# Feed-forward up-projection by Strassen's seven block products, two weight slabs at a time

## The chip, the cores and the metric

The kernel runs on one core of a Trainium2 chip. The metric is device time of one execution in microseconds; the runs shown here have a median of 1751.15 us.

## The reference

One step of a streaming encoder of two layers. Its 512 prompt frames and 64 sample frames are computed together as 576 token columns, D_MODEL = 1024. Layer 0 mixes tokens by chunked band attention, layer 1 by a Mamba-2 scan; each is followed by a dense feed-forward part with 4096 hidden units, and each of these four sublayers by a residual and a layer norm:

```python
def _mlp(x, w_up, w_down):
    return (jnp.square(jax.nn.relu(x @ w_up)) @ w_down)
x = layer_norm(ALPHA * x + mixer(x))
x = layer_norm(ALPHA * x + _mlp(x, w_up, w_down))
```

All inputs and outputs are float32.

## The kernel before

**Layout and split.** Activations lie transposed, features on 128 partitions in 8 blocks, tokens along the free axis (`x32`, 128 x 8 x 576). Every large matrix product is done as three products of rounded halves: an operand is cast to the type fp32r (its high part), and the rest, operand minus high part, is cast too (its low part). A product of 128 outputs over a 1024-deep sum is 8 blocks x 3 terms (high by high, high by low, low by high), each in two token halves of 288: 48 matmuls. `dense` (L229) does both halves, `dense_half` (L251) one half for two weight slabs.

**Weights.** The weights come as 223 slabs of 128x1024 f32 in the order of `weight_plan` (L66). `Weights.load` (L128) takes a raw buffer (two of them, tag `wr`), issues the DMA on SP's queue, casts the high part on ScalarE (L144) and makes the low part on VectorE, or on GpSimd for slabs near the head of a stage (`pool_lo`, L146). High and low parts have NB = 6 buffers each. `get` asks for slabs up to LA = 4 ahead, `drop` tells that one is used up.

**The feed-forward stage** (`mlp`, L385). The 4096 hidden units are four groups q of eight tiles. `up(q)` makes eight tiles of 128 hidden units, each with Relu and Square on ScalarE (L392, L394), the copy that is the high part and the low part on VectorE (L395, L399). `down(q)` takes a group's eight tiles as its sum axis and adds to the residual stream, eight slabs (`resid`, L297, an add from PSUM on VectorE). The order is up 0, up 1, down 0, up 2, down 1, up 3, down 2, down 3. At the start LAG = 5 tiles are computed for the first token half, while the second half's layer norm of the stage before still runs beside them as a generator (`Side`, `layer_norm` L315) stepped by every 7 matmuls; then the same five for the second half. At the end the last LAG tiles of `down(3)` are done by halves in the same way, so that the first half's norm runs beside the second half's matmuls.

**Order.** The kernel is written in a framework that takes buffers from pools by tag, puts in the waits between engines, and sets the order of each engine's instructions when the program is built. An engine runs its own instructions in that fixed order. PSUM for the large products is two buffers of two banks each (tag `mm`).

## Time and profile before

| | us |
|---|---|
| median of 3 runs | 1751.15 (1749.54 to 1751.87) |
| the profiled execution | 1747.71 |
| its span, first to last instruction | 1745.9 |
| TensorE busy | 1698.6 (97%) |
| VectorE busy | 952.5 (55%) |
| ScalarE busy | 658.5 (38%) |
| GpSimd busy | 298.5 (17%) |

The mean granted clock of TensorE is 0.987 of full speed. Matmuls are pipelined, so TensorE's busy share is the share of time with a matmul under way; a matmul's own time (298 ns) overlaps the next. In the profile PE is TensorE, PEld its weight load, DVE VectorE, ACT ScalarE, POOL GpSimd, SP the queue that issues DMAs; L236 is line 236 of the kernel.

### The profile page before, as it was taken

The numbers are of one execution on the slowest core, as the hardware profiler recorded it, in microseconds if no ns is written. First come the engines' busy times: TensorE is split into PE (matmuls) and PEld (weight loads), VectorE is DVE, ScalarE is ACT, GpSimd is POOL, SyncE is SP. The second block draws the span as 40 slices with busy tenths as digits, with TensorE's granted clock in tenths as the row PEclk, the third lists the DMA queues.
The fourth block names the chain that finished last, engine by engine and source line by source line (L and its number), as shares of the span: only waits on it lengthen the run. The fifth ranks groups of instructions, "written<-read, shape, count | busy, mean of one in ns | idle before, by whom it ended". The sixth has DMA issues, their size and how long they took to land.

```text
span 1745.9 us, 30837 instructions
## 1 busy us (share of the span) xinstructions
PE 1698.6 (97%) x12857; PEld 1625.7 (93%) x12857; DVE 952.5 (55%) x1728; ACT 658.5 (38%) x1084; POOL 298.5 (17%) x343
## 2 busy tenths in 40 slices
PE   9999999899999999999999999999989999999995
PEld 8888888799999999988999999999989999999995
DVE  6555555853333333377875776777777333333326
ACT  5434442453122231145563563565226322313102
POOL 0000011400000000434441341344340000000011
PEclk9999999999999999999999999999989999999998
DMA  7343331122222222112432332333212222222211
GB/s 241 115 127 104 103 118 56 61 94 77 84 85 85 85 76 82 61 60 91 142 101 86 100 106 82 98 106 103 64 59 73 85 85 86 81 77 85 85 37 54
DMA packets 76922, 157.21 MB, mean 90 GB/s; under 512 B 11440, under 2 KB 40240, under 8 KB 76784
## 3 DMA queue, kind: packets, MB, share of 16 engines
q1 hardware_dynamic: 76784, 155.25, 27.7%
q8 instruction: 101, 1.65, 0.4%
q14 instruction: 37, 0.30, 0.1%
HBM read 145.80 MB, written 9.42 MB: 89 GB/s over the span
## 4 chain that ended last, share of the span: by engine, by line
PE 89%; DVE 7%; ACT 1%; issue 1%; POOL 1%; DMA 0%; POOLq 0%; DVEq 0%; SPq 0%; ACTq 0%
PE mm L236 73%; PE mm L258 3%; PE ax L596 1%; DVE tmp L332 1%; PE ax L618 1%; PE ax L901 1%; PE ax L904 1%; PE ax L567 1%; PE ax L906 1%; PE ax L292 1%; DVE x L325 1%; PE mm L247 1%; PE ax L577 1%; PE ax L282 1%; PE ax L870 1%
## 5 line engine op out<-in xcount | busy, mean ns | idle before, releaser
L144 ACT CAST wh<-wr 128x1024 fp32r<-128x1024 f32 x223 | 233.5, 1047 | 630.5 <-PE mm L236 602.8
L236 PE MATMUL mm<-xh,wh 128*128 128x288 f32 x1920 | 416.5, 298 | 0.1
L236 PE MATMUL mm<-xh,wl 128*128 128x288 f32 x1920 | 415.3, 298 | 0.0
L236 PE MATMUL mm<-xl,wh 128*128 128x288 f32 x1920 | 414.4, 297 | 0.0
L146 DVE TENSOR_TENSOR wl<-wr,wh 128x1024 fp32r<-128x1024 f32 x196 | 249.6, 1274 | 266.9 <-ACT wh L144 263.4
L236 PEld LDWEIGHTS mm<-xl,wh 128*128 128x128 f32 x1920 | 308.1, 189 | 4.1 <-issue 3.8
L236 PEld LDWEIGHTS mm<-xh,wh 128*128 128x128 f32 x1920 | 308.8, 189 | 2.7 <-issue 1.1
L236 PEld LDWEIGHTS mm<-xh,wl 128*128 128x128 f32 x1920 | 308.3, 189 | 1.4
L236 PE MATMUL mm<-hh,wl 128*128 128x288 f32 x1024 | 242.2, 298 | 0.0
L236 PE MATMUL mm<-hh,wh 128*128 128x288 f32 x1024 | 242.1, 298 | 0.0
L236 PE MATMUL mm<-hl,wh 128*128 128x288 f32 x1024 | 241.8, 297 | 0.0
L304 DVE TENSOR_TENSOR x<-x,mm 128x288 f32<-128x288 f32 (+1 forms) x112 | 65.1, 581 | 223.3 <-PE mm L236 223.0
L236 PEld LDWEIGHTS mm<-hh,wh 128*128 128x128 f32 x1024 | 173.5, 190 | 0.1
L236 PEld LDWEIGHTS mm<-hl,wh 128*128 128x128 f32 x1024 | 173.4, 190 | 0.0
L236 PEld LDWEIGHTS mm<-hh,wl 128*128 128x128 f32 x1024 | 173.3, 189 | 0.1
L146 POOL TENSOR_TENSOR wl<-wr,wh 128x1024 fp32r<-128x1024 f32 x27 | 66.7, 2472 | 440.4 <-ACT wh L144 435.2
L712 DVE SCALAR_TENSOR_TENSOR tmp<-xpad,pm,tmp 128x579 f32<-128x579 f32 x90 | 90.2, 1002 | 2.8 <-ACT tmp L710 2.0
L313 POOL TENSOR_TENSOR tmp<-x 128x288 f32<-128x288 f32 x8 | 6.8, 855 | 387.5 <-DVE x L304 384.6
L258 PE MATMUL mm<-xh,wh 128*128 128x288 f32 x240 | 71.2, 297 | 0.5 <-DVE x L304 0.5
L258 PE MATMUL mm<-xl,wh 128*128 128x288 f32 x240 | 71.4, 298 | 0.1
L258 PE MATMUL mm<-xh,wl 128*128 128x288 f32 x240 | 70.8, 295 | 0.0
L302 DVE SCALAR_TENSOR_TENSOR x<-x,mm 128x576 f32<-128x576 f32 (+1 forms) x34 | 24.4, 719 | 83.7 <-PE mm L236 83.5
(216 smaller groups left out, 2448.8 us busy)
## 6 DMA issues: line engine op xcount, KB each, us to landing
wr<-in_wts SPq DMA_DIRECT2D x223, 512.0 KB, 3.3
cumb<-cumd SPq DMA_DIRECT2D x32, 256.0 KB, 3.8
e<-expd SPq DMA_DIRECT2D x48, 64.0 KB, 3.5
tb<-in_rel SPq DMA_DIRECT2D x16, 160.0 KB, 3.7
tb<-in_rel SPq DMA_DIRECT2D x16, 144.0 KB, 3.0
ts<-in_rel SPq DMA_DIRECT2D x16, 144.0 KB, 2.9
out_k<-tmp SPq DMA_DIRECT2D x8, 288.0 KB, 2.3
out_v<-tmp SPq DMA_DIRECT2D x8, 288.0 KB, 2.1
```

The lines of the kernel that those rows point to most:

```text
L144: S.copy(hi[:, sl], raw)
L146: eng.tensor_tensor(out=lo[:, sl], in0=raw, in1=hi[:, sl].bitcast(F32), op=ALU.subtract)
L236: PE.matmul(ps[:, o:o + HALF], w, a(k)[:, t0:t0 + HALF], start=first and i == 0, stop=last and i == 2)
L247: PE.matmul(ps[:, PS0 + h * HALF:PS0 + (h + 1) * HALF], a, b[:, k, h * HALF:(h + 1) * HALF], start=k == 0 and i == 0, stop=k == 7 and i == 2)
L258: PE.matmul(o, a, b[:, k, h * HALF:(h + 1) * HALF], start=k == 0 and i == 0, stop=k == 7 and i == 2)
L282: PE.matmul(ps[0:96, j:j + 1], vv[:, 96 * j:96 * j + 96], scale_col, start=True, stop=True)
L292: PE.matmul(ps[:, 96 * j:96 * j + 96], y[:, j0 + j:j0 + j + 1].to_broadcast([96, 128]), ident[0:96, 0:96], start=True, stop=True)
L302: V.scalar_tensor_tensor(out=dst, in0=dst, scalar=ALPHA, in1=src, op0=ALU.mult, op1=ALU.add)
L304: V.tensor_tensor(out=dst, in0=dst, in1=src, op=ALU.add)
L325: V.tensor_tensor(out=r, in0=r, in1=pmu[:, 0:HALF].unsqueeze(1).to_broadcast([P, 2, HALF]), op=ALU.subtract)
L332: V.tensor_tensor(out=acc, in0=acc, in1=sq, op=ALU.add)
L712: V.scalar_tensor_tensor(out=acc, in0=xr[:, k:k + 579], scalar=col(k), in1=acc, op0=ALU.mult, op1=ALU.add)
```

## The change

The up-projection of two neighbouring slabs (256 hidden units, tokens in two halves, the sum axis in two halves of 512) is seen as a 2x2 by 2x2 block product and done with seven block products of four 128-blocks each instead of eight (a Winograd form of Strassen's scheme). The first four tiles of a stage (LAG is now 4) are still done by halves as before; the other 28 tiles of a layer are 14 pairs.

- Weight sums: the second operand slabs of a pair are made in place in the raw buffers by four GpSimd subtractions and additions of 128x512; a pair's four weight operands (three of 1024 columns, one of 512) are each split into high and low part.
- Token sums: t1 to t4 of `x32` are made once a stage, on VectorE with ScalarE casts, t2 to t4 (`combos`) as a side generator beside the second half of the first four tiles, t1 (`first_combo`) behind them, in place of the second half of blocks 0 to 3 of `xh`, `xl`.
- Results: four blocks of a pair are put together in an SBUF tile `ut` by three ScalarE copies and four VectorE adds from PSUM; three of the seven products go on accumulating in a bank that was copied or added before. Relu, Square and the split run once over 1152 columns.
- Order: up pairs and down groups interleave by `MLP_ORDER`; the last `down(3)` begins with two slabs together, their last two blocks behind.
- Buffers: NB 6 to 5, four raw buffers with DMAs issued ahead (`prefetch`), LAG 5 to 4, `pool_lo` from i-3 to i+3 instead of i+5, hidden tiles as five pair buffers instead of two groups of eight.

The diff, cut to its core:

```diff
-NB = 6
-LAG = 5
+NB = 5
+NR = 4
+LAG = 4
+HALFK = 512
 LA = 4
 PL0 = -3
-PL1 = 6
+PL1 = 4
 WARM = 7
 HE = 17
 DE = 40
-ACTM = 1
 LN_EVERY = 7
+CE = 12
...
+MLP_ORDER = (("up", 0, LAG // 2, 4), ("up", 1, 0, 1), ("down", 0, 0, 8), ("up", 1, 1, 4), ("up", 2, 0, 1),
+             ("down", 1, 0, 8), ("up", 2, 1, 4), ("up", 3, 0, 1), ("down", 2, 0, 8), ("up", 3, 1, 4),
+             ("down", 3, 0, 8))
+
+
...
+        p = [("up", layer, 0, m) for m in range(LAG)]
+        for kind, q, i0, i1 in MLP_ORDER:
+            if kind == "up":
+                p += [("ups", layer, q, i, g) for i in range(i0, i1) for g in (1, 2, 4, 3)]
+            else:
+                p += [("down", layer, q, m) for m in range(8)]
...
+            def prefetch(self):
+                while self.raw_done < min(self.raw_free + NR, self.n_raw):
+                    raw = wp.tile([P, 1024], F32, name="wr", tag="wr", bufs=NR)
+                    SY.dma_start(raw, io["wts"][self.raw_done])
+                    self.raw[self.raw_done] = raw
+                    self.raw_done += 1
 
             def load(self, upto):
-                while self.done < min(upto, len(plan)):
-                    i = self.done
-                    raw = wp.tile([P, 1024], F32, name="wr", tag="wr", bufs=2)
-                    hi, lo = self.alloc()
-                    self.fetch(i, raw, hi, lo, 0, 1024)
-                    self.t[i] = (hi, lo)
+                while self.done < min(upto, self.live + NB, len(plan)):
+                    self.prefetch()
+                    self.produce(self.done)
                     self.done += 1
 
             def alloc(self):
                 return (wp.tile([P, 1024], F32R, name="wh", tag="wh"),
                         wp.tile([P, 1024], F32R, name="wl", tag="wl"))
+
+            def split(self, i, raw, n=1024):
+                hi, lo = self.alloc()
+                S.copy(hi[:, 0:n], raw)
+                eng = GP if i in pool_lo else V
+                eng.tensor_tensor(out=lo[:, 0:n], in0=raw, in1=hi[:, 0:n].bitcast(F32), op=ALU.subtract)
+                self.t[i] = (hi, lo)
+
+            def produce(self, i):
+                p = plan[i]
+                r = self.raw_free
+                if p[0] != "ups":
+                    self.split(i, self.raw.pop(r))
+                    self.raw_free += 1
+                    return
+                r1, r2 = self.raw[r], self.raw[r + 1]
+                lo, hi = slice(0, HALFK), slice(HALFK, 1024)
+                if p[4] == 1:
+                    self.split(i, r1)
+                    GP.tensor_tensor(out=r2[:, lo], in0=r1[:, lo], in1=r2[:, lo], op=ALU.subtract)
+                elif p[4] == 2:
+                    self.split(i, r2)
+                    GP.tensor_tensor(out=r2[:, hi], in0=r2[:, hi], in1=r2[:, lo], op=ALU.subtract)
+                    GP.tensor_tensor(out=r1[:, lo], in0=r1[:, lo], in1=r2[:, hi], op=ALU.add)
+                    GP.tensor_tensor(out=r2[:, lo], in0=r1[:, hi], in1=r2[:, hi], op=ALU.subtract)
+                elif p[4] == 4:
+                    self.split(i, r1[:, lo], HALFK)
+                else:
+                    self.split(i, r2)
+                    del self.raw[r], self.raw[r + 1]
+                    self.raw_free += 2
+                    self.prefetch()
 
...
+        def dense_ks(ps, wf, ah, al, ks):
+            for k in ks:
+                wh, wl = wf(k)
+                for i, (w, a) in enumerate(((wh, ah), (wh, al), (wl, ah))):
+                    for t0 in (0, HALF):
+                        PE.matmul(ps[:, PS0 + t0:PS0 + t0 + HALF], w, a(k)[:, t0:t0 + HALF],
+                                  start=k == 0 and i == 0, stop=k == 7 and i == 2)
 
...
+                th = hpool.tile([P, 12, HALF], F32R, name="th")
+                tl = hpool.tile([P, 12, HALF], F32R, name="tl")
                 H = {}
+                T1, T2 = slice(0, HALF), slice(HALF, NT)
...
+                def combine(dh, dl, t):
+                    S.copy(dh, t)
+                    V.tensor_tensor(out=dl, in0=t, in1=dh.bitcast(F32), op=ALU.subtract)
+
+                def sums_of(kk):
+                    t = tmp().rearrange("p (a b) -> p a b", a=2)
+                    return t, slice(2 * kk, 2 * kk + 2), slice(4 + 2 * kk, 6 + 2 * kk)
+
+                def combos():
+                    for kk in range(2):
+                        t3, k1, k2 = sums_of(kk)
+                        V.tensor_tensor(out=t3, in0=x32[:, k2, T2], in1=x32[:, k1, T2], op=ALU.subtract)
+                        combine(th[:, 4 + 2 * kk:6 + 2 * kk, :], tl[:, 4 + 2 * kk:6 + 2 * kk, :], t3)
+                        yield
+                        t2, k1, k2 = sums_of(kk)
+                        V.tensor_tensor(out=t2, in0=t3, in1=x32[:, k1, T1], op=ALU.add)
+                        combine(th[:, k1, :], tl[:, k1, :], t2)
+                        yield
+                        t4, k1, k2 = sums_of(kk)
+                        V.tensor_tensor(out=t4, in0=x32[:, k2, T1], in1=t2, op=ALU.subtract)
+                        combine(th[:, 8 + 2 * kk:10 + 2 * kk, :], tl[:, 8 + 2 * kk:10 + 2 * kk, :], t4)
+                        yield
+
+                def first_combo():
+                    for kk in range(2):
+                        t1, k1, k2 = sums_of(kk)
+                        V.tensor_tensor(out=t1, in0=x32[:, k1, T2], in1=x32[:, k1, T1], op=ALU.subtract)
+                        combine(xh[:, k1, T2], xl[:, k1, T2], t1)
+
+                operands = {
+                    "b11": lambda k: (xh[:, k, T1], xl[:, k, T1]),
+                    "b21": lambda k: (xh[:, 4 + k, T1], xl[:, 4 + k, T1]),
+                    "b22": lambda k: (xh[:, 4 + k, T2], xl[:, 4 + k, T2]),
+                    "t1": lambda k: (xh[:, k, T2], xl[:, k, T2]),
+                    "t2": lambda k: (th[:, k, :], tl[:, k, :]),
+                    "t3": lambda k: (th[:, 4 + k, :], tl[:, 4 + k, :]),
+                    "t4": lambda k: (th[:, 8 + k, :], tl[:, 8 + k, :]),
+                }
+
+                def product(out, w, off, name, more=False):
+                    for k in range(4):
+                        wh, wl = (x[:, off + 128 * k:off + 128 * k + 128] for x in w)
+                        bh, bl = operands[name](k)
+                        for i, (a, b) in enumerate(((wh, bh), (wh, bl), (wl, bh))):
+                            PE.matmul(out, a, b, start=not more and k == 0 and i == 0, stop=k == 3 and i == 2,
+                                      skip_group_check=True)
+
+                def up_pair(q, i):
+                    hpair(q, i)
+                    w1, w2, w4, w3 = (W.get("ups", layer, q, i, g) for g in (1, 2, 4, 3))
+                    ab, cd = mmt(), mmt()
+                    a, b = ab[:, 0:HALF], ab[:, 512:512 + HALF]
+                    c, d = cd[:, 0:HALF], cd[:, 512:512 + HALF]
+                    ut = hpool.tile([P, 4, HALF], F32, name="ut", tag="ut", bufs=2)
+                    add = lambda dst, src: V.tensor_tensor(out=dst, in0=dst, in1=src, op=ALU.add)
+                    product(a, w1, 0, "b11")
+                    S.copy(ut[:, 0, :], a)
+                    product(b, w1, HALFK, "b21")
+                    add(ut[:, 0, :], b)
+                    W.drop()
+                    W.load(W.pos + 2)
+                    product(d, w2, 0, "t3")
+                    S.copy(ut[:, 3, :], d)
+                    product(c, w4, 0, "t1")
+                    add(ut[:, 3, :], c)
+                    product(a, w3, HALFK, "t2", True)
+                    S.copy(ut[:, 1:3, :], a.unsqueeze(1).to_broadcast([P, 2, HALF]))
+                    add(ut[:, 3, :], a)
+                    product(d, w2, HALFK, "t4", True)
+                    W.drop(2)
+                    W.load(W.pos + 4)
+                    product(c, w3, 0, "b22", True)
+                    add(ut[:, 1:3, :], cd.rearrange("p (a b) -> p a b", a=2)[:, :, 0:HALF])
+                    W.drop()
+                    W.load(W.pos + 4)
+                    u = ut.rearrange("p a b -> p (a b)")
+                    S.activation(u, u, AF.Relu)
+                    S.activation(u, u, AF.Square)
+                    hh, hl = (x.rearrange("p a b -> p (a b)") for x in H[q, i])
+                    V.tensor_copy(hh, u)
+                    V.tensor_tensor(out=hl, in0=u, in1=hh.bitcast(F32), op=ALU.subtract)
+
...
+                            side.start(combos(), CE)
...
+                    side.drain()
+                    first_combo()
...
+                        w2 = [W.get("down", layer, q, m) for m in range(2)]
+                        p2 = [mmt(), mmt()]
+                        for ks in (range(0, 6), range(6, 8)):
+                            for w, ps in zip(w2, p2):
+                                dense_ks(ps, wk(w), bh, bl, ks)
+                        for m, ps in enumerate(p2):
+                            for h in range(2):
+                                resid(ps, m, (h,), False, True)
+                            W.drop()
+                        for m in range(2, 8 - LAG):
```

## Rows read from the trace of the kernel before

**Rows 1.** The page's busy time, share and instructions of an engine.
```profile
PE 1698.6 (97%) x12857; PEld 1625.7 (93%) x12857; DVE 952.5 (55%) x1728; ACT 658.5 (38%) x1084; POOL 298.5 (17%) x343
```

**Rows 2.** Chain of waits, whole span: start us, us, what.
```profile
369.29 363.50 PE mm L236 x2726
```

**Rows 3.** Busy time by engine in the feed-forward stretch of layer 0.
```profile
369.30:732.80 363.50, 363.50 (x2727) 363.50 (x2727) 122.03 (x148) 92.00 (x112) 14.38 (x12) 1.00 0.25 83
```

**Rows 4.** Groups of instructions, 400 to 725 us (busy us, mean ns).
```profile
L146 DVE TENSOR_TENSOR wl<-wr,wh 128x1024 fp32r<-128x1024 f32 x47 | 57.6, 1226 | 93.1 <-ACT wh L144 91.7
L399 DVE TENSOR_TENSOR hl<-tmp,hh 128x576 fp32r<-128x576 f32 x23 | 17.5, 759 | 0.8
L304 DVE TENSOR_TENSOR x<-x,mm 128x576 f32<-128x576 f32 x16 | 12.1, 755 | 67.2 <-PE mm L236 67.2
L395 DVE CAST hh<-tmp 128x576 fp32r<-128x576 f32 x23 | 10.6, 461 | 1.0
L304 DVE TENSOR_TENSOR x<-x,mm 128x288 f32<-128x288 f32 x9 | 4.1, 455 | 23.1 <-PE mm L236 23.1
...
L144 ACT CAST wh<-wr 128x1024 fp32r<-128x1024 f32 x50 | 52.4, 1047 | 237.3 <-PE mm L236 237.3
L394 ACT ACTIVATE tmp<-tmp 128x576 f32<-128x576 f32 x23 | 15.8, 687 | 0.7
L392 ACT ACTIVATE tmp<-mm 128x576 f32<-128x576 f32 x23 | 14.8, 645 | 0.0
```

**Rows 5.** GpSimd's source lines: duration ns min/median/max.
```profile
L146 POOL TENSOR_TENSOR wl<-wr,wh x27: 2337/2395/2934, 249.3 to 1316.3; 128x1024 fp32r<-128x1024 f32 x27
...
L873 POOL TENSOR_TENSOR mt<-cumb,cumt x40: 606/1040/1772, 820.4 to 1238.5; 128x512 f32<-128x512 f32 x32, 64x256 f32<-64x256 f32 x8
...
L875 POOL TENSOR_TENSOR mt<-mt,negm x40: 724/1294/2139, 821.5 to 1239.2; 128x512 f32<-128x512 f32 x32, 64x256 f32<-64x256 f32 x8
```

**Rows 6.** Order of time near 313 us (start, us, instruction), line 332's durations.
```profile
312.54 2.40 POOL L146 TENSOR_TENSOR wl<-wr,wh 128x1024 fp32r<-128x1024 f32 x1 [3.43 <-ACT wh L144]
312.71 0.45 DVE L302 SCALAR_TENSOR_TENSOR x<-x,mm 128x288 f32<-128x288 f32 x1
313.08 2.47 DVE L332 TENSOR_TENSOR tmp<-tmp 128x576 f32<-128x576 f32 x1
...
L332 DVE TENSOR_TENSOR tmp<-tmp x24: 735/758/2480, 313.1 to 1731.3; 128x576 f32<-128x576 f32 x24
```

**Rows 7.** Order of time, ScalarE (in brackets idle before, releaser).
```profile
420.33 1.05 ACT L144 CAST wh<-wr 128x1024 fp32r<-128x1024 f32 x1 [4.09 <-PE mm L236]
421.28 0.64 ACT L392 ACTIVATE tmp<-mm 128x576 f32<-128x576 f32 x1
```

**Rows 8.** Order of time, TensorE and VectorE, start of layer 0's feed-forward stage.
```profile
333.36 0.29 PE L258 MATMUL mm<-xh,wh 128*128 128x288 f32 x1
347.65 0.81 PE L292 MATMUL ax<-pm,y 96*128 96x96 f32 x6
...
351.52 1.59 DVE L357 TENSOR_TENSOR xl<-x,xh 128x576 fp32r<-128x576 f32 x2
356.84 0.76 DVE L357 TENSOR_TENSOR xl<-x,xh 128x576 fp32r<-128x576 f32 x1 [0.63 <-ACT xh L356]
```

**Rows 9.** Order of time, TensorE and VectorE, layer 0's end of feed-forward.
```profile
749.19 1.12 PE L292 MATMUL ax<-pm,y 96*128 96x96 f32 x6 [2.01 <-DVE y L277]
...
753.65 0.75 DVE L357 TENSOR_TENSOR xl<-x,xh 128x576 fp32r<-128x576 f32 x1
756.87 0.75 DVE L357 TENSOR_TENSOR xl<-x,xh 128x576 fp32r<-128x576 f32 x1
```

**Rows 10.** Order of time, TensorE after a wait.
```profile
326.22 1.39 PE L292 MATMUL ax<-pm,y 96*128 96x96 f32 x6 [3.81 <-DVE y L277]
...
327.95 0.44 PE L236 MATMUL mm<-oh,wl 128*128 128x288 f32 x1
328.19 0.44 PE L236 MATMUL mm<-oh,wh 128*128 128x288 f32 x1
```

More of the change, by code (lines that the diff above doesn't have):

```diff
@@ L63, with slab_plan @@
 GORD = (("c", 0), ("z", 0), ("b", 0), ("x", 0), ("x", 1), ("z", 1))
+MLP_ORDER = (("up", 0, LAG // 2, 4), ("up", 1, 0, 1), ("down", 0, 0, 8), ("up", 1, 1, 4), ("up", 2, 0, 1),
+             ("down", 1, 0, 8), ("up", 2, 1, 4), ("up", 3, 0, 1), ("down", 2, 0, 8), ("up", 3, 1, 4),
+             ("down", 3, 0, 8))
+def slab_plan():
+    slabs = []
+    for p in weight_plan():
+        if p[0] != "ups":
+            slabs.append(p)
+        elif p[4] == 1:
+            slabs += [("up", p[1], p[2], 2 * p[3] + j) for j in range(2)]
+    return slabs
 def weight_plan():
@@ L72, in mlp @@
     def mlp(layer):
-        p = []
-        for kind, q in (("up", 0), ("up", 1), ("down", 0), ("up", 2), ("down", 1), ("up", 3),
-                        ("down", 2), ("down", 3)):
-            p += [(kind, layer, q, m) for m in range(8)]
+        p = [("up", layer, 0, m) for m in range(LAG)]
[4 more added lines that the diff above has]
+                p += [("down", layer, q, m) for m in range(8)]
         return p
@@ L144, in fetch @@
                 S.copy(hi[:, sl], raw)
-                eng = GP if i in pool_lo else V
-                eng.tensor_tensor(out=lo[:, sl], in0=raw, in1=hi[:, sl].bitcast(F32), op=ALU.subtract)
+                V.tensor_tensor(out=lo[:, sl], in0=raw, in1=hi[:, sl].bitcast(F32), op=ALU.subtract)
             def load_first(self, load_x):
@@ new lines, in first_tiles @@
+                def first_tiles():
+                    ws = []
+                    for i in range(LAG // 2):
+                        hpair(0, i)
+                    for h in range(2):
+                        if h == 0:
+                            side.start(layer_norm(ln_in, 1, False), LN_EVERY)
+                        else:
+                            side.drain()
+                            side.start(combos(), CE)
+                        for m in range(0, LAG, PAIR_UP):
+                            ms = range(m, min(m + PAIR_UP, LAG))
+                            if h == 0:
+                                ws += [W.get("up", layer, 0, i) for i in ms]
+                            for i, src in zip(ms, dense_half(ws[m:m + PAIR_UP], h)):
+                                act(src, 0, i, h * HALF, (h + 1) * HALF)
+                                if h == 1:
+                                    W.drop()
+                    side.drain()
+                    first_combo()
@@ L461, in down @@
                             side.drain()
-                up(0)
-                up(1)
-                down(0)
-                up(2)
-                down(1)
-                up(3)
-                down(2)
-                down(3)
+                first_tiles()
+                for kind, q, i0, i1 in MLP_ORDER:
+                    if kind == "up":
+                        for i in range(i0, i1):
+                            up_pair(q, i)
+                    else:
+                        down(q)
         def attention():
@@ L674, in attention @@
                 ya = [yt[k] for k in range(4)]
[L675 removed]
+                out_chunk("wo", 0, ya, True, 3)
                 side.drain()
                 yb = [yt[k] for k in range(4, 8)]
[L678 removed]
+                out_last("wo", [(0, mp, ya, True, False) for mp in range(3, 4)]
                          + [(1, mp, yb, False, True) for mp in range(4)], 0)
@@ L1005, in kt @@
         return w.reshape(-1, 128, w.shape[1]).transpose(1, 0, 2).reshape(128, -1)
-    out = np.empty((len(weight_plan()), 128, 1024), np.float32)
-    for i, s in enumerate(weight_plan()):
+    out = np.empty((len(slab_plan()), 128, 1024), np.float32)
+    for i, s in enumerate(slab_plan()):
         if s[0] == "v":
```

64 lines of the change are left out of this document (21 added, 43 removed).

## The prediction

> **What bounds the kernel now.** I read the busy table first: TensorE is busy for 1698.6 of 1745.9 us, GpSimd for 17% [rows 1]. Then the chain of waits: it crosses each feed-forward stage as one unbroken piece of matmuls, 363.50 us for 2726 of them in layer 0 [rows 2], so 133.3 ns a matmul; the piece of layer 1 looks the same. In the stretch by engine of layer 0, VectorE works 122.0 and ScalarE 92.0 of 363.5 us at a granted clock of 1.00 [rows 3]. So inside the feed-forward stages TensorE alone sets the time, and a matmul less is worth 133 ns, as long as the other engines stay behind it. At the two ends of each stage it is the layer norm that PE waits for, and there the price of a change is another.
>
> **What is removed.** A pair of weight slabs takes 2 x 48 = 96 matmuls of 128x288 now and 7 products x 4 blocks x 3 split terms = 84 after the change; the shape, the weight load and the type of each are the same. Pairs that change: (32 - 4) / 2 = 14 a layer, 28 in all. 28 x 12 = 336 matmuls, x 133.3 ns = **44.8 us**. A pair falls from 12.8 to 11.2 us. This is the whole gain: the time can't fall below it.
>
> **What is added for a pair**, by rows of the same operations [rows 4]:
> - ScalarE: 3.5 casts of a slab instead of 2, 3.5 x 1.047 = 3.7; three PSUM copies (288, 288 and 576 columns; Relu from PSUM takes 0.645 for 576, and for half of that I take 0.4, between half and all of it) 1.45; Relu and Square over 1152 columns, which no row shows: 0.69 to 1.38 each by one or two times the 576 row; I take 1.2. Sum 7.5 of 11.2 us.
> - VectorE: 3.5 low parts x 1.226 = 4.3; three adds of 288 x 0.455 and one of 576 x 0.755 = 2.1; the copy and the low part of the squares over 1152 columns, between one and two times 0.461 and 0.759, I take 0.8 and 1.4. Sum 8.6 of 11.2 us.
> - GpSimd: four sums of 128x512. Its rows for that shape are 1.04 and 1.29 us, and half of its 128x1024 low part is 1.2 [rows 5]. The sums are in place, like the 1.29 row; I take 1.25, so 5.0 us (4.2 to 5.2).
>
> By sums alone all of it hides behind 11.2 us. Two things speak against that.
>
> First, *GpSimd and VectorE get in each other's way.* While GpSimd ran 2.40 us from 312.54, a VectorE add of two SBUF tensors that began at 313.08 took 2.47 us; its shortest time is 0.735. An add with one operand in PSUM, begun at 312.71 in the same GpSimd instruction, took its usual 0.45 [rows 6]. So low parts and copies from SBUF (6.5 us a pair) and the sums (5.0) exclude each other: 11.5 us against a pair of 11.2.
> The Trainium skill, page "SBUF — State Buffer", section "Who interferes with whom", says that VectorE with two SBUF inputs and GpSimd with reads share one port pair, taken for a whole instruction, the other blocked. The 2.47 beside 0.735 us agrees. If the port were never idle or fought for, the pair would by that page be 0.3 us longer, an estimate; in turn, full speed side by side would make the price nothing.
>
> Second, *chains.* The order on an engine is not program order. In the stage's steady state the cast of a weight slab runs at 420.33, when the matmuls release its buffer, and Relu of the tile just finished follows at 421.28, although the program issues that Relu first: with six buffers, the slab that takes a buffer just released is the one six places on, and the program asks for it only two tiles later [rows 7]. So the order is by when work could start. I lay out a run of pairs by that rule (zero is the start of the run's first pair, whose weights were made during the eight down slabs ahead):
> - Pair 0: products end at 1.6, 3.2, 4.8 and so on to 11.2. The buffer of the next second weight comes free at 3.2, its cast ends at 4.35, its low part at 5.6; then three sums one behind the other, to 9.5; cast of the last sum to 10.75 and its low part to about 12.0 to 12.7, because GpSimd's next sum holds VectorE up. The last add of c and d follows, to 13.4, then Relu, Square, copy and low part of the squares, some 5 us.
> - Pair 1: these 5 us lie on ScalarE and VectorE just where the next second weight wants them. Its low part ends 8.6 us into the pair, not 5.6. No product waits yet (add of c has to end by 20.8, and ends at 20.3).
> - Pair 2: the third sum's low part ends near 29.8, wanted by the fifth product at 28.8: 1 us late. Pair 3: some 1.2 more.
> Runs between two down stages have 3, 4, 4 and 3 pairs: 1.0 + 2.2 + 2.2 + 1.0 = 6.4 us a layer, **12.8 us** in all. Bounds: nothing (all hidden), and for a chain that closes on itself 3.2 us in each of the later pairs (a rival below). Less than nothing is excluded, as PE has no gap in these stretches to win back.
>
> **LAG 5 to 4** shortens the cover of the layer norms by one tile of a half, 24 matmuls = 3.2 us, in three places and the tail.
> - Start of both feed-forward stages: the first tiles start at 333.36, the statistics are spread at 347.65, and the low parts of the second half's blocks 0 to 3 end at 353.1 (two instructions, the first at about 352.3), the last at 357.6 [rows 8]. Four tiles of 3.2 us, and some 4 us of the norm's own matmuls and waits among them, bring PE to the second half at about 350.0 instead of 353.2: it waits until 352.3, and some 0.6 more at the later blocks. 2.9 us a stage, 5.8 in all.
> - Feed-forward 0 into the state-space stage: broadcast at 749.19, the first low part done at 754.4 [rows 9], the next two by 757.6. Of the 36 matmuls that lay behind the broadcast 12 are left. They end near 753; then PE waits 1.4 us for the first blocks and about 1.6 for the later ones: 3.0 us.
> - Tail: the last norm's first half comes out later by about 1 us.
> Sum **9.8 us**, bounds 4 (half of the waits met by other order) and 13 (four times 3.2). A gap costs more than its length where the clock falls: after PE's wait of 3.81 us the matmuls at 327.95 and 328.19 are 0.24 us apart [rows 10] instead of 0.133: the lower of the clock's two levels, 1.2 instead of 2.4 GHz. My gaps are shorter, so I add nothing.
>
> **Token sums.** Six sums in the second half of the first tiles and two behind it: 8 x (0.76 + 0.76) = 12.2 us of VectorE and 8 x 0.65 = 5.2 of ScalarE a stage (576 columns each). VectorE has there besides the squares of four half tiles (3.0), the rest of the norm (3) and the pair's low parts (4.3): 22.5 us, in 12.8 us of matmuls and the 8 us until the sixth product needs t4. It is late by about 2 us a stage, **4 us** in all (0 to 8). Their matmuls' first operands lie in x and t3, which come first.
>
> **Costed at nothing.** One weight buffer less: a slab was cast up to six slabs (38 us) ahead, five are 32. Four raw buffers instead of two: DMAs start sooner, and PE waits for none now. The two down slabs begun together give the last pair 72 matmuls, 9.6 us, to be squared. If that cover were gone, 5 us a layer. SP issues the same 223 slab DMAs in the same order, and GpSimd's queue has nothing else in these stages until the norm's sums.
>
> **Sum.** -44.8 + 12.8 + 9.8 + 4.0 = -18.2 us on the profiled execution (1747.71, of which 1745.9 span): 1729.5. The median of the runs is 1751.15, 3.4 above; the same difference gives **1733**. About 0.2%, 3.5 us, is what a measurement of this kernel can tell from no change.
>
> **Rivals.**
> 1. *All hidden in the pairs.* For it: busy sums of 8.6 and 7.5 of 11.2 us, and that the down slabs refill the buffers every 3 or 4 pairs. Against it: 11.5 us on what VectorE and GpSimd exclude. 1751.15 - 44.8 + 9.8 + 0 = 1716.
> 2. *The chain closes (slower).* If VectorE's fixed order has the last weight's low part, then the add of c and d, then the squares, then the next first weight, one round is 1.23 + 3 x 1.25 + 1.05 + 1.23 + 0.75 + 1.2 + 1.2 + 0.8 + 1.4 + 1.23 + 0.46 = 14.3 us against 12.8 before. Laid out so, a run of four pairs takes 51.9 us (51.2 before), one of three 37.5 (38.4); that gives back all 44.8. It decides from the second pair on, at the third product, which can't overwrite d before the add has read it. 1751 + 9.8 + 4 = 1765. Against it: rows 7, where a later cast goes ahead.
> 3. *The exclusion is the bound.* VectorE's PSUM adds (2.1) don't overlap with sums, 11.5 + about 1.3 = 12.8 a pair: no gain in the pairs, and some of the 13.8 at the ends won back by LAG's lighter load: 1751 to 1760. The 0.45 us of the add from PSUM [rows 6] speaks against the full price. The Trainium skill's rule on the shared port pair, named above, is the mechanism.
> 4. *Not what it says.* Products reopened on a sum that was already read could cost PE more than 133 ns; at 152 ns nothing is won. No row speaks for it: the order of operands is as now.
>
> **Chances.** Forecast (1722 to 1744) 0.45; rival 1 0.25; rival 2 0.16; rival 3 0.10; rival 4 0.04. Faster: the first two and a few points of rival 3, 0.73. Same 0.07. Slower 0.20. The range reaches from below rival 1 to just short of rival 2: 1711 to 1760; the forecast's own is 1722 to 1744.
>
> **What would show it.** Right: 336 matmuls fewer; products in chunks of 12 at 133 ns; the pair stretch of a first pair at 11.2 us and of a third or fourth at 12 to 12.5; VectorE low parts with a maximum near 2.4 us while GpSimd adds; PE waits at the first matmul of the second half, 2 to 3 us. Wrong: pairs at 11.2 throughout (rival 1); PE waiting for the add of c and d in each pair (rival 2); sums on GpSimd over 1.5 us, which would lengthen the chain by 1 us a pair.

## The result: 1.25% slower

The changed kernel takes 1773.05 us (median of 4, 1771.72 to 1775.52) against 1751.51 (1749.54 to 1752.99): ratio 1.0125, interval 1.0108 to 1.0143. The forecast was 1733, the range 1711 to 1760.

The page's busy times after the change (before: [rows 1]):

```profile
PE 1683.3 (95%) x12521; PEld 1592.3 (90%) x12521; DVE 1090.8 (62%) x1874; ACT 744.1 (42%) x1182; POOL 445.0 (25%) x449
```

The 336 matmuls are gone (12857 - 12521), yet the span grew from 1745.9 to 1772.6 us. The chain of waits is cut where it was one piece of 363.50 us [rows 2]; here is the second run of four pairs, in order of time (start, us, what):

```profile
467.93 16.52 PE mm L514 x118
486.20 2.24 DVE wl L173
495.46 3.35 PE mm L514 x22
508.75 3.34 PE mm L514 x22
512.63 6.74 PE mm L514 x48
519.37 51.20 PE mm L294 x384
```

A down group keeps its 51.20 us for 384 matmuls. The pairs start and stop. Busy times of that run of four, in the form of [rows 3] (start and end, us, then busy us and count of PE, PEld, VectorE, ScalarE, GpSimd, the granted clock, and the share and GB/s of the DMA engines):

```profile
467.76:519.21 51.45, 47.57 (x338) 45.12 (x337) 33.06 (x38) 26.85 (x34) 14.55 (x11) 1.00 0.28 86
```

336 matmuls at 133.3 ns are 44.8 us; the run takes 51.45, and eight plain tiles took 51.2. VectorE works 33 of 51 us: no engine is full. What PE waits for, from the first pair of layer 0 on (total us, times, longest):

```profile
PE mm L514 <- DVE ut L524: 23.5, 37, 1.6
...
PE mm L514 <- ACT tmp L465: 9.5, 2, 4.8
```

One round of the steady state, all engines in order of time, with the plain PE rows left out:

```profile
500.48 1.22 DVE L173 TENSOR_TENSOR wl<-wr,wh 128x1024 fp32r<-128x1024 f32 x1
501.78 1.29 POOL L190 TENSOR_TENSOR wr<-wr 128x512 f32<-128x512 f32 x1 [9.37 <-DVE wl L173]
...
504.39 1.29 POOL L192 TENSOR_TENSOR wr<-wr 128x512 f32<-128x512 f32 x1
...
505.71 2.00 ACT L171 CAST wh<-wr 128x1024 fp32r<-128x1024 f32 x2 [0.62 <-POOL wr L192]
...
506.80 1.23 DVE L173 TENSOR_TENSOR wl<-wr,wh 128x1024 fp32r<-128x1024 f32 x1 [0.57 <-ACT wh L171]
507.95 0.75 DVE L524 TENSOR_TENSOR ut<-ut,mm 128x576 f32<-128x576 f32 x1
...
508.73 1.17 ACT L546 ACTIVATE ut<-ut 128x1152 f32<-128x1152 f32 x1 [1.02 <-DVE ut L524]
...
508.75 0.40 PE L514 MATMUL mm<-th,wh 128*128 128x288 f32 x1 [1.05 <-DVE ut L524]
```

This is the closed chain: second weight's low part (500.48), three sums, cast, low part of the last weight (506.80), and only behind it the add of c and d (507.95), which frees the bank of the next third product (508.75). Relu and Square follow, then high and low part of the squares, and behind these VectorE makes the next second weight. A second branch closes at the same time: the chain of waits above goes through PE's 22 matmuls behind the wait (3.34 us) and the add of b, which stands between the two parts of the squares on VectorE. At 512.1 both branches are there, within 0.1 us. The same wait stands at 495.46: a round is 13.29 us, against 12.8 for two plain tiles.

PE also starts up more slowly behind such a wait: the matmul ahead of the one at 508.75 and the one behind it start 1.32 us further apart than two at 133 ns, for a wait of 1.05. Over the six waits of this run the difference is 0.25 to 0.28 us each, 0.26 taken below.

**Where the spans differ** (PE's landmarks in both traces, us):

| part | forecast | measured |
|---|---|---|
| 336 matmuls x 133.3 ns | -44.8 | -44.8 |
| pairs behind a down group, 2 x (4 + 4 + 3), above 11.2 each | 10.8 | 33.2 |
| both stages from first matmul to first down slab: LAG, token sums, first three pairs | 11.8 | 36.2 |
| ends of the stages | 4.0 | 0.1 |
| ahead of layer 0's stage (+3.5), state space (-1.6) | 0 | 1.9 |
| sum | -18.2 | 26.6 |

The third row is 416.56 - 336.84 = 79.7 and 1403.40 - 1322.22 = 81.2 us for ten tiles, against 106.2 and 104.9 for sixteen, less six tiles of 6.4 and three pairs' gain of 1.6. It lies 24.4 us above the forecast, the second row 22.4.

### The profile page after: what moved, and what is told of

It reads as the page before. It is cut to its first block, busy times and chain, and to the rows that moved or that the text cites. A ratio compares the mean times of both kernels' runs of the same rounds, so it can differ in the third digit from the quotient of the medians.

```text
span 1772.6 us, 30745 instructions
## 1 busy us (share of the span) xinstructions
PE 1683.3 (95%) x12521; PEld 1592.3 (90%) x12521; DVE 1090.8 (62%) x1874; ACT 744.1 (42%) x1182; POOL 445.0 (25%) x449
## 4 chain that ended last, share of the span: by engine, by line
PE 80%; DVE 10%; POOL 3%; ACT 3%; issue 2%; DMA 1%; SPq 0%; DVEq 0%; ACTq 0%; POOLq 0%
PE mm L294 51%; PE mm L514 12%; PE mm L324 3%; DVE wl L173 2%; PE ax L748 1%; PE mm L303 1%; ACT wh L171 1%; PE ax L1053 1%; PE ax L770 1%; PE ax L1056 1%; DVE tmp L398 1%; PE ax L719 1%; PE ax L358 1%; PE ax L1058 1%; DVE hl L550 1%
## 5 line engine op out<-in xcount | busy, mean ns | idle before, releaser
L171 ACT CAST wh<-wr 128x1024 fp32r<-128x1024 f32 (+1 forms) x279 | 279.4, 1006 | 508.0 <-PE mm L294 363.7
L173 DVE TENSOR_TENSOR wl<-wr,wh 128x1024 fp32r<-128x1024 f32 (+1 forms) x258 | 322.7, 1252 | 95.5 <-ACT wh L171 91.9
L294 PE MATMUL mm<-xh,wl 128*128 128x288 f32 x1056 | 231.6, 300 | 0.0
L294 PE MATMUL mm<-xh,wh 128*128 128x288 f32 x1056 | 230.8, 300 | 0.1
L294 PE MATMUL mm<-xl,wh 128*128 128x288 f32 x1056 | 230.8, 299 | 0.0
L294 PEld LDWEIGHTS mm<-xl,wh 128*128 128x128 f32 x1056 | 169.3, 189 | 4.1 <-issue 3.8
L294 PEld LDWEIGHTS mm<-xh,wh 128*128 128x128 f32 x1056 | 169.7, 189 | 2.4 <-issue 1.4
L294 PEld LDWEIGHTS mm<-xh,wl 128*128 128x128 f32 x1056 | 169.6, 189 | 1.6
L514 PE MATMUL mm<-th,wh 128*128 128x288 f32 x336 | 106.3, 316 | 33.1 <-DVE ut L524 23.5
L514 PE MATMUL mm<-xh,wh 128*128 128x288 f32 x448 | 136.5, 305 | 0.6 <-ACT ut L532 0.6
L514 PE MATMUL mm<-xl,wh 128*128 128x288 f32 x448 | 133.5, 298 | 0.3 <-DVE xl L472 0.3
L514 PE MATMUL mm<-xh,wl 128*128 128x288 f32 x448 | 133.3, 298 | 0.0
L514 PE MATMUL mm<-tl,wh 128*128 128x288 f32 x336 | 99.7, 297 | 0.0
```

The source lines that it names most:

```text
L171: S.copy(hi[:, 0:n], raw)
L173: eng.tensor_tensor(out=lo[:, 0:n], in0=raw, in1=hi[:, 0:n].bitcast(F32), op=ALU.subtract)
L294: PE.matmul(ps[:, o:o + HALF], w, a(k)[:, t0:t0 + HALF], start=first and i == 0, stop=last and i == 2)
L514: PE.matmul(out, a, b, start=not more and k == 0 and i == 0, stop=k == 3 and i == 2, skip_group_check=True)
```

## Experiments

Theory A: the closed chain above, held by VectorE's fixed order. Rival B: GpSimd and VectorE exclude each other, so the work doesn't fit. Each run is given with its ratio to the kernel before on the same chip, and its first run of four pairs behind a down group (51.45 in the changed kernel).

**1. Without the sums** (the four `GP.tensor_tensor` lines of `produce` left out).

> The changed kernel takes 1773.05 us. Leaves out the four GpSimd sums of each pair, so the products use the raw slabs; all else stays. Theory A (a closed round: low part of the second weight, three GpSimd sums, cast, low part of the last weight, add of c and d, squares, next second weight, held together by VectorE's fixed order): the waits of the third product for the add of c and d go, 11.2 us a layer with the refill behind each wait (0.39 + 1.58 + 1.05 in a run of four pairs, 1.08 in the last run of three), so 22.3 us in all and perhaps some of the 4.8 us at each first pair: 1745 to 1752. Rival B (GpSimd and VectorE exclude each other; the load, not the dependence): gains about as much here, 1745 to 1755. Rival C (reopened products or the other waits are what costs): 1768 to 1775.

1742.99 us, ratio 0.9965 (0.9952 to 0.9977): 28 us under the changed kernel by ratio. A run of four takes 47.47, and the first three pairs of a stage 40.4 and 39.7 us (45.2 and 45.3 in the changed kernel). Both theories allow that; the time is 2 us under both of their ranges.

**2. The sums on a scratch tile**, same shapes, same engine:

```diff
-GP.tensor_tensor(out=r2[:, lo], in0=r1[:, lo], in1=r2[:, lo], op=ALU.subtract)
+GP.tensor_tensor(out=self.gs, in0=r1[:, lo], in1=r2[:, lo], op=ALU.subtract)
```
(all four alike)

> The four sums of a pair stay on GpSimd with the same shape, at the time the raw slabs arrive, but write a scratch tile, so that no weight depends on them (the products use the raw slabs). Theory A: the round is open though GpSimd works as long as before; the waits of the third product go, 1745 to 1753, within 4 us of the kernel without sums. Rival B (exclusion): the waits stay, as GpSimd takes the port for as long: 1768 to 1775.

1764.07 us, 1.0088 (1.0069 to 1.0107): between the two. The stretch decides. Run of four of the kernel without sums, then of this one:

```profile
460.19:507.66 47.47, 46.62 (x338) 45.00 (x337) 30.88 (x38) 27.18 (x34) 0.00 (x0) 1.00 0.28 93
```
```profile
474.70:523.32 48.62, 46.82 (x339) 45.03 (x338) 33.71 (x38) 27.18 (x34) 12.78 (x8) 1.00 0.27 91
```

GpSimd's 12.8 us cost 1.15 us in a run; the dependence costs 51.45 - 48.62 = 2.83. So in this run A is about 70% of what the sums cost, B 30%. The split is rough: the sums run at other times here than in the changed kernel, 8 instead of 11 GpSimd instructions in the stretch. And this kernel's first tiles took 44.1 and 41.8 us (34.6 and 35.8 in the changed kernel): its sums all run as the raw slabs land, in the middle of the norm and token sums, and this ate the gain. GpSimd, then PE, at the first tiles of layer 0:

```profile
339.70 0.79 POOL L379 TENSOR_TENSOR tmp<-tmp,x 128x288 f32<-128x288 f32 x1
```
```profile
340.54 0.75 PE L387 MATMUL ax<-tmp,invd 128*128 128x288 f32 x2 [4.43 <-POOL tmp L379]
```

PE waits 4.43 us for the norm's own last sum, which stands behind two of the scratch sums (335.59 and 338.48) in GpSimd's order; the changed kernel has no such wait in its first tiles. Part of the loss is thus GpSimd's order and not exclusion; how much was not measured.

**3. VectorE's order alone**: the last two low parts queued behind the add of c and d.

```diff
-                    W.load(W.pos + 4)
                     product(c, w3, 0, "b22", True)
-                    add(ut[:, 1:3, :], ...)
+                    last = add(ut[:, 1:3, :], ...)
                     W.drop()
-                    W.load(W.pos + 4)
+                    with tc.issue_after(last.ins):
+                        W.load(W.pos + 4)
```

> The same instructions as the changed kernel; only VectorE's order differs: the low parts of the next pair's third and last weights stand behind the add of c and d, not ahead of it. Theory A: the third product no longer waits for that add: 1773.05 - 22.3 = 1751 (1747 to 1757; ScalarE's order still has the last weight's cast ahead of Relu, which may keep part of the round). Rival B: the same work and the same exclusion, so no difference: 1769 to 1775.

1761.03 us, 1.0068 (1.0053 to 1.0083). The third product's wait went, as A says; half of the gain came. The first run of four takes 49.80 (all four: 48.65 to 50.78), with one wait, at the second product, for ScalarE's copy of a. ScalarE ahead of it, then PE:

```profile
488.50 0.62 ACT L171 CAST wh<-wr 128x512 fp32r<-128x512 f32 x1 [2.15 <-POOL wr L191]
489.75 2.00 ACT L171 CAST wh<-wr 128x1024 fp32r<-128x1024 f32 x2 [0.63 <-POOL wr L192]
491.65 1.16 ACT L546 ACTIVATE ut<-ut 128x1152 f32<-128x1152 f32 x1
492.72 0.38 ACT L526 COPY ut<-mm 128x288 f32<-128x288 f32 x1
```
```profile
493.15 0.40 PE L514 MATMUL mm<-xh,wh 128*128 128x288 f32 x1 [1.89 <-ACT ut L526]
```

The casts stand in line for GpSimd and hold Relu and the copy behind them: the round closes over ScalarE instead. From 494.2 to 497.5 the matmuls then start 0.24 us apart, the 1.2 GHz level, which costs 1.5 us of the 49.80:

```profile
465.40:515.20 49.80, 47.89 (x339) 46.44 (x338) 28.81 (x36) 26.85 (x34) 13.31 (x11) 0.97 0.24 85
```

**4. Sums apart**: the first difference of the second half goes to a 128x512 tile `ws` of its own, so that no sum waits for the second weight's low part.

```diff
-GP.tensor_tensor(out=r2[:, hi], in0=r2[:, hi], in1=r2[:, lo], op=ALU.subtract)
-GP.tensor_tensor(out=r1[:, lo], in0=r1[:, lo], in1=r2[:, hi], op=ALU.add)
-GP.tensor_tensor(out=r2[:, lo], in0=r1[:, hi], in1=r2[:, hi], op=ALU.subtract)
+GP.tensor_tensor(out=ws, in0=r2[:, hi], in1=r2[:, lo], op=ALU.subtract)
+GP.tensor_tensor(out=r1[:, lo], in0=r1[:, lo], in1=ws, op=ALU.add)
+GP.tensor_tensor(out=r1[:, hi], in0=r1[:, hi], in1=ws, op=ALU.subtract)
```
(all four sums now stand behind the split of the first weight; the last weight is split in two halves)

> The sums no longer wait for the low part of the second weight: the first difference of the second half goes to a tile of its own, so the four sums run when the raw slabs and the first weight's low part are there, two thirds of a pair earlier (cost: the last weight is split in two halves, one cast and one low part more). Theory A: the round is open, 1773.05 - 22.3 + 0 = 1751 (1747 to 1756). Rival B: GpSimd and VectorE work and exclude as before, 1769 to 1777.

1754.57 us, 1.0037 (1.0024 to 1.0051); runs of four 48.88 to 48.90. In the first run of four no wait for the add of c and d is left, without an order set by hand. One wait of 1.13 us stays, for the add of c, which stands behind a low part that took 2.31 us beside a GpSimd sum. A holds, B's 1769 doesn't.

**5. LAG 5 to 4 in the kernel before** (`LAG = 4`, nothing else).

> The kernel before with one edit, LAG 5 to 4. The prediction's term: +9.8 in all (2.9 at each feed-forward start, 3.0 at the end of feed-forward 0, 1 in the tail). What the trace of the changed kernel showed instead: at a feed-forward start 2.08 + 0.93 us of waits, 0.26 behind each until matmuls overlap again, and 3.4 us at half the clock (1.5 us lost), so 5.0 a start, and nothing at the ends; here the attention's last part also loses one tile of cover, which the changed kernel kept (0 to 3). So 1751.5 + 10 + 0 to 3 = 1761 to 1765, with first tiles 5 us longer against four of the five tiles of before. Rival (the norm's matmuls or token sums, not LAG, make the first tiles long): 1751 to 1757.

1758.41 us, 1.0050 (1.0035 to 1.0064), +8.7 against a forecast of 9.8, and a little under the 10 to 13 that were expected here. Nearly all of it lies at the starts (first matmul to first down slab 110.51 and 110.51, before 106.23 and 104.87), nothing at the end of layer 0's stage (111.78, before 111.94). In the changed kernel the same place reads:

```profile
355.78 0.40 PE L324 MATMUL mm<-xh,wh 128*128 128x288 f32 x1 [2.08 <-DVE xh L420]
357.11 0.40 PE L324 MATMUL mm<-xl,wh 128*128 128x288 f32 x1 [0.93 <-DVE xl L423]
...
358.54 0.44 PE L324 MATMUL mm<-xl,wh 128*128 128x288 f32 x1
358.78 0.44 PE L324 MATMUL mm<-xh,wl 128*128 128x288 f32 x1
```

The waits are the forecast 2.9 us (3.01). Behind them matmuls start 0.24 us apart, the 1.2 GHz level, from 358.3 to 361.7: 1.5 us more.

**6. Without the token sums** (the products read blocks of x).

> The changed kernel without the token sums t1 to t4 (the products read blocks of x in their place). Theory: the 4.75 us wait of the first pair's third product for a token sum's cast, the refill and the half clock behind it (4.9 + 0.27 + 1.7 = 6.9 a stage) are the token sums' price: 1773.05 - 14 = 1759 (1756 to 1763); the waits at the second half of the first tiles stay. Rival (the weight sums of the first pair hold the same engines up anyway): 1768 to 1774.

1764.09 us, 1.0082 (1.0065 to 1.0099), 7.5 less than the changed kernel by ratio. The first three pairs fall from 45.16 and 45.34 to 39.43 and 39.56 us, 11.5 in all; 2.6 of it came back at the norms (1.0 at the end of layer 0's stage, 1.6 in the state space stage). My reading of the 4.75 us wait as one for a token sum's cast was wrong. ScalarE and VectorE of the changed kernel ahead of that matmul, then PE:

```profile
371.30 0.62 ACT L171 CAST wh<-wr 128x512 fp32r<-128x512 f32 x1 [2.52 <-POOL wr L191]
373.75 0.67 ACT L471 CAST th<-tmp 128x576 fp32r<-128x576 f32 x1 [1.84 <-DVE tmp L485]
...
377.43 0.40 ACT L465 ACTIVATE tmp<-mm 128x288 f32<-128x288 f32 x1
```
```profile
370.04 3.01 DVE L468 TENSOR_TENSOR hl<-tmp,hh 128x288 fp32r<-128x288 f32 x2
```
```profile
377.88 0.61 PE L514 MATMUL mm<-th,wh 128*128 128x288 f32 x1 [4.75 <-ACT tmp L465]
```

The third product waits for a Relu of the last first tile, and this stands behind a weight cast that waits for a GpSimd sum and a token cast that waits for VectorE, which lies blocked beside GpSimd (3.01 us for two low parts of 288 columns; the same two took 0.81 at 378.96, with GpSimd idle).

**7. Sums apart, with the copies of a and d written behind the second and fourth product.**

```diff
-                    S.copy(ut[:, 0, :], a)
                     product(b, w1, HALFK, "b21")
+                    S.copy(ut[:, 0, :], a)
```
(and the copy of d behind `product(c, w4, ...)`)

> The kernel with sums apart, with two copies moved: the copy of a is written behind the second product, that of d behind the fourth, so that no product into the other bank of the same tile has to wait for a read. TensorE's order becomes first, second, third, fourth, fifth product. Theory: the wait at the second or fifth product (0.28 us and 0.26 us until matmuls overlap again, in nearly every pair) goes: 1754.6 - 28 x 0.5 = 1741 (1737 to 1746), a run of four pairs from 48.9 to 46.9 or less. Rival (the copies then come late and Relu with them): 1752 to 1757.

1775.99 us, 1.0150 (1.0123 to 1.0176): 20 us slower than sums apart, a run of four 51.23. The add of b now fell behind the low part of the squares on VectorE, and that beside GpSimd took 2.33 us instead of 1.35:

```profile
485.12 2.33 DVE L556 TENSOR_TENSOR hl<-ut,hh 128x1152 fp32r<-128x1152 f32 x1
487.38 0.44 DVE L530 TENSOR_TENSOR ut<-ut,mm 128x288 f32<-128x288 f32 x1
```

PE waits 1.31 us for that add. So order again, made worse by B.

**8. The same, with LAG 5 at the start**, a sixth tile computed plainly and 13 pairs a layer.

> As the kernel with late copies, with the first part of the stage laid out anew: LAG back to 5 with five weight buffers, the sixth tile computed plainly for both halves, 13 pairs a layer instead of 14 (+1.6 us a layer), and t1 made behind the sixth tile. Theory: the 5.0 us of each start (waits for the second half's norm with clock) go, and the token sums have 6.4 us more cover, worth 2 to 4: 2 x (5.0 + 3 - 1.6) = 13 below the kernel with late copies: 1728 (1722 to 1736). Rival (five buffers held by five first tiles leave the sixth tile's and the first pair's weights late): 1738 to 1750.

1754.80 us, 1.0033 (1.0020 to 1.0046): 21 less than experiment 7, where 13 were expected. Runs of four stay at 51.2. Of the spans' difference of 25.0 us, 16.4 lie between the first matmul of a stage and its first down slab, 7.9 in the state space stage. Why that one got shorter was not followed.

**9. Experiment 8 with the order by hand.** Products 1, 3, 2, 4, 5, 6, 7; the adds of b, c, and of c and d ahead of what else waits on VectorE, Relu and Square ahead of the next first weight's cast:

```diff
+                    ab2 = add(ut[:, 0, :], b)
+                    with tc.issue_after(ab2.ins):
+                        while pend:
+                            pend.pop()()      # low part of the squares of the pair before
...
+                    with tc.issue_after(ac.ins):       # ac: add of c
+                        W.load(W.pos + 2)
+                    with tc.issue_after(p4.ins):       # p4: last matmul of the fourth product
+                        product(a, w3, HALFK, "t2", True)
...
+                    with tc.issue_after(last.ins):     # last: add of c and d
+                        W.load(W.pos + 4)
...
+                    with tc.issue_after(sq.ins):       # sq: Square
+                        W.load(W.pos + 5)
```

> The kernel with sums apart and the LAG 5 start, with the order fixed by hand: products first, third, second, fourth, fifth, sixth, seventh, so that each copy or add has another product beside it; on VectorE the add of b ahead of the low part of the squares, the add of c ahead of the next second weight's low part, the add of c and d ahead of the last weight's; on ScalarE Relu and Square ahead of the next first weight's cast. Theory (fixed order, not the amount of work, makes the stalls; the sums' exclusion takes about 1 us of a run of four): a run of four pairs 46.5 us (45.5 to 48) against 51.2, the last three pairs 34.5 against 37.3, the first two 25 against 28.5: 1754.8 - 31 = 1724 (1716 to 1735). Rival B (GpSimd's sums and VectorE's SBUF work can't fit beside each other in a pair): a run of four stays at 49 or more, 1742 to 1757.

1730.50 us, 0.9879 (0.9860 to 0.9898). The run of four:

```profile
456.52:503.71 47.19, 45.84 (x339) 44.84 (x337) 33.60 (x40) 27.10 (x37) 15.33 (x9) 1.00 0.28 91
```

As much VectorE and GpSimd work as in the changed kernel (33.6 and 15.3 against 33.1 and 14.6 us), 4.26 us less, and 0.3 less than without any sums (1). B's "49 or more" falls. The 1730.50 has more in it than the order: LAG 5, and 13 pairs a layer.

**10. The same with the high part of the squares on ScalarE** (`S.copy(hh, u)`).

> As the kernel with the order by hand, with the high part of the squares (1152 columns) copied on ScalarE instead of VectorE: 0.8 us less VectorE a pair, 1.2 more ScalarE. If VectorE's time with the exclusion is what is left: 4 to 8 us faster than the kernel with the order by hand. If order is settled: within 3 us of it. If ScalarE is now late (its copies of a and d gate products): 3 to 15 us slower.

1733.68 us, 0.9904 (0.9886 to 0.9921); a run of four 48.19. Less work on VectorE gained nothing, so its amount isn't the limit. The run is 1.0 us longer, and its three waits (0.92, 0.73 and 0.92 us) are now for a copy on ScalarE: the third of the readings expected.

**11. Experiment 9 without low parts on GpSimd** (`PL1 = -3`).

> As the kernel with the order by hand, with no low part on GpSimd at the stage heads (21 slabs go to VectorE, 1.23 instead of 2.4 us each). Theory (exclusion also strikes the layer norm: a 96x3 VectorE step took 2.26 us instead of 0.16 beside a GpSimd low part, the next 1.19 beside the first weight sum): the norm's chain ahead of each stage gets up to 3 us shorter, so 4 to 9 us faster than the kernel with the order by hand. Rival (21 low parts more on VectorE, 26 us at stage heads where it is busiest, cost what they give): within 3 us, or slower.

1725.65 us, 0.9856 (0.9840 to 0.9873). VectorE, GpSimd and PE of the changed kernel at the norm ahead of layer 0's stage:

```profile
325.17 2.26 DVE L342 SCALAR_TENSOR_TENSOR w<-w,v 96x3 f32<-96x3 f32 x1
327.46 1.19 DVE L343 SCALAR_TENSOR_TENSOR y<-w,y 96x3 f32<-96x3 f32 x1
```
```profile
325.07 2.34 POOL L173 TENSOR_TENSOR wl<-wr,wh 128x1024 fp32r<-128x1024 f32 x1
327.37 1.26 POOL L187 TENSOR_TENSOR wr<-wr 128x512 f32<-128x512 f32 x1
```
```profile
328.71 1.60 PE L358 MATMUL ax<-pm,y 96*128 96x96 f32 x6 [4.86 <-DVE y L343]
```

And of this experiment, the matching VectorE steps and PE:

```profile
324.87 0.16 DVE L347 SCALAR_TENSOR_TENSOR w<-w,v 96x3 f32<-96x3 f32 x1
325.06 0.65 DVE L348 SCALAR_TENSOR_TENSOR y<-w,y 96x3 f32<-96x3 f32 x1
```
```profile
325.77 0.91 PE L363 MATMUL ax<-pm,y 96*128 96x96 f32 x6 [1.15 <-DVE y L348]
```

Three columns take 2.26 us because GpSimd began 0.1 us earlier. The kernel before had the first of the two (PE waits 3.81 [rows 10]); the first weight sum added the second. This is 1.05 of the 3.5 us that the changed kernel lost ahead of the stage; 1.0 more lies behind the wait, most of it because more matmuls there run at the 1.2 GHz level, and 1.4 had been lost before 297 us, which was not followed. The Trainium skill, "SBUF — State Buffer", section "Who interferes with whom", calls the shared port pair an exclusive lock; these rows agree, for instructions of 0.16 us too. The gain is 3.2 us there, 4.4 at the end of layer 0's stage and 2.6 in the state space stage; 6.3 were lost at the start of layer 1's stage.

**12. The changed kernel with nothing but the order by hand** (sums in place, LAG 4).

> The changed kernel (sums in place, LAG 4, low parts on GpSimd) with nothing but the order by hand of products, adds, squares and casts. Theory: the engines' order is what closes the round; with it opened the in-place sums still reach ScalarE (the last weight's cast, which waits for three sums, stands ahead of Relu), some 0.5 us a pair. A run of four pairs 47.5 to 49.5 us instead of 51.4, the last three 35 to 36, 1773 - 23 = 1750 (1744 to 1758). Rival (the in-place sums close the round whatever the order on the other engines): runs of four at 50.5 or more, 1763 to 1775.

1778.60 us, 1.0165 (1.0139 to 1.0190); runs of four 51.5 to 52.0. My expectation falls; the runs are as the rival says, the time is 3.6 us above its range. ScalarE, then VectorE:

```profile
494.73 0.62 ACT L171 CAST wh<-wr 128x512 fp32r<-128x512 f32 x1 [3.81 <-POOL wr L191]
```
```profile
495.38 1.11 DVE L173 TENSOR_TENSOR wl<-wr,wh 128x512 fp32r<-128x512 f32 x1 [3.06 <-ACT wh L171]
496.42 0.74 DVE L527 TENSOR_TENSOR ut<-ut,mm 128x576 f32<-128x576 f32 x1
```

Here it is the third weight's low part, which waits for two sums, that stands ahead of the add of c and d: in my order only the last weight's was behind it. With sums that start late, something that waits for them always stands ahead of the adds; to start them early (4) and then to order the adds (9) are both needed.

**13. Experiment 11 with low parts on GpSimd at the start of layer 1's stage alone.**

> As the kernel without low parts on GpSimd, but with them at the head of feed-forward 1 alone, where their absence cost 6 us (from its first matmul to the first down slab 76.0 us against 69.7 with them). If the two heads are independent: 1725.65 - 6 = 1720 (1717 to 1724). If that head's 6 us came from elsewhere (the norm ahead of it): 1724 to 1729.

1723.29 us, 0.9838 (0.9825 to 0.9851), the lowest median here, though its interval overlaps that of experiment 11. That start took 69.71 us again (76.01 without), but the state space stage ahead of it grew from 549.15 to 554.90. The two heads are not independent: a GpSimd low part helps the stage that it feeds and holds up the norm that it runs beside. At that norm PE waits 3.84 us for `y` behind a VectorE step of 2.26 us that began 0.1 us after a GpSimd low part of 2.34; experiment 11 has no wait for `y` there. But 1.4 of the 5.8 us arose far earlier, beside no such low part. Not tried: other places for the first weight sums.

## Why the prediction was wrong

**The step that failed** is the second point under "What is added for a pair", *chains*: "So the order is by when work could start", with 1.0 to 2.2 us a run. The sizes in it were right (sums 1.29 us each where 1.25 was taken, Relu and Square 1.17, squares 0.76 and 1.35); its layout of pair 0 adds 0.1 to 0.2 us between engines without saying so (4.35 for 3.2 + 1.05, 10.75 for 9.5 + 1.05), which changes nothing here. The order was not. From one row, a cast ahead of a Relu [rows 7], I took it that a ready instruction is never held by one that is not. But an engine's order is fixed when the program is built, and in it the last weight's low part stands ahead of the add of c and d, whether its sums have come or not. Rival 2 is this mechanism: it said 51.9 and 37.5 us for runs of four and three, and 51.4 and 37.1 (the last run of a layer) were measured; it gave 1765 at a chance of 0.16. I had its price and held rows 7 against it. For the runs behind a down group the step gave 10.8 us, and 33.2 were measured.

**A term put at nothing.** Not all of the 33.2 us is the sums' round. Without the sums (1) the same runs still lie 15.0 us above 11.2 a pair: nearly every pair waits for the add of b, and PE starts late at changes of product. The prediction has no term for that. The order by hand (9) leaves 11.4 us, next to the 10.8 forecast, but for these other reasons: that agreement is luck.

**LAG.** 9.8 forecast, 8.7 measured alone (5), but in other places: at the starts the waits are as computed and the clock adds 1.5 us; at the ends nothing. "My gaps are shorter, so I add nothing" was wrong: two gaps of 2.08 and 0.93 us were followed by 3.4 us at the 1.2 GHz level.

**Token sums and first pair.** 4.0 forecast; without them the first runs are 11.5 shorter (6). VectorE was nearly full there, as forecast (busy 20.7 of the 22.1 us from 355.78 to 377.90); that ScalarE's Relu would queue behind casts waiting for GpSimd and VectorE was not seen. Taken one by one, LAG (9.9 us at the starts by the landmarks of 5), token sums (11.5, 6) and weight sums (10.4 less in the first three pairs, 1) come to 31.8 of the third row's 36.2 us. Whether they overlap is not shown.

**Costed at nothing.** The prediction saw "nothing else" on GpSimd's queue until the norm's sums, and missed that the pair's first sum runs beside the norm ahead of the stage: 1 us there, and the clock after it. "One weight buffer less" stays open. In the steady state the second weight's cast starts when PE lets a buffer go, 0.7 us before VectorE is free for the low part:

```profile
498.71 1.05 ACT L171 CAST wh<-wr 128x1024 fp32r<-128x1024 f32 x1 [0.75 <-PE mm L514]
```

Whether a sixth buffer would have started the round earlier was not tried.

**What held.** 336 matmuls at 133 ns; the products themselves run at full speed (rival 4 falls: 47.2 us for a run of four is 140 ns a matmul, waits included); exclusion of VectorE and GpSimd costs, but 1.15 us in a run of four, not all of the gain (rival 3 falls as a bound). The scheme can give a time like the forecast: 1730.5 us with sums apart, order by hand and LAG 5 at the start.

The 33.2 us of the second row of the table, by PE's gaps: 10 waits for the add of c and d, 12.7 us by their rows; 3 waits for an add of c alone, 1.2 us, behind a low part that took 2.3 us beside GpSimd; 16 waits for the add of b at 0.28, 4.5 us; and 0.26 behind each of the 29, 7.5. The other 7 us lie at other changes of product, eight of 0.09 to 0.24 us in the run shown, and stay open.

## What to carry to other kernels

Before counting busy time, write down each engine's order through one round and ask of every instruction that waits for another engine what stands behind it; a chain that closes over two fixed orders sets the period however idle the engines are. An operand that another engine has to make should start from data that is there early, at the price of a buffer, before the order is touched. And work on GpSimd is not free beside a chain of small VectorE steps.

## What was not expected of the hardware

- A VectorE instruction of 0.16 us took 2.26 us beside a GpSimd one of 2.34; the reverse holds too: a GpSimd sum of 1.29 us had a mean of 2.00 at one of its lines in experiment 2.
- In the pairs a wait of PE cost its length and 0.26 us more. After waits of 2.08 and 0.93 us with one matmul between them, 3.4 us at the 1.2 GHz level followed, while after single waits of 1.05 and 1.58 in the pairs the granted clock stayed at 1.00. The length of a wait alone doesn't decide: in experiment 3 one of 1.89 us was followed by the lower level (clock of the run 0.97), one of 1.94 us in the next run was not (1.00).
